# The last FFN norm of a two-layer trunk: its row sums of squares are taken from the turned residual

## Chip, cores and metric

One core of a Trainium2 chip runs the whole program. The metric is the device time of one execution in microseconds: the kernel before took 966.81 us, the median of three runs (966.55 to 966.98).

## What is computed

A decoder trunk of two layers over 512 tokens of 1024 channels, in float32. Each layer adds a mixer and a gated FFN to the residual `h`, each behind an RMS norm:

```
def rms_norm(x, g):
    y = x32 * lax.rsqrt(jnp.mean(x32 * x32, axis=-1, keepdims=True) + EPS)
    return y.astype(x.dtype) * g
...
for layer in range(DEPTH):
    xn = rms_norm(h, norm_mix[layer])
    ...
    h = h + jnp.einsum('bse,ed->bsd', mix, w_out_odd[i])
    hn = rms_norm(h, norm_ffn[layer])
    h = h + gated_conv_ffn(hn, w_ffn_gate[layer], w_ffn_up[layer], ...)
return rms_norm(h, final_norm)
```

The case is about the last `norm_ffn`, that of layer 1: the sum over 1024 channels of the squares of `h`, for each of 512 tokens.

## The kernel before, in words

The residual lies turned: `h[k]` (k = 0 to 7) holds 128 channels on the partitions and all 512 tokens along the free dimension. Every float32 product is made from two parts of each operand, a rounded one (`hi`) and the rest (`lo`), in three matmuls (L156 to L158, or L705 in the FFN's and the projections' block products). ACT makes `hi`; `lo` is made by VectorE as a subtraction (L152, L202, L857), or by ACT and an adding DMA on GpSimd's queue (L141 and L143, L822 to L824).

A `Norm` multiplies h by its gain (`add`, L199, into the pair `hg[k]`) and squares it: ACT squares each `h[k]` (L208, L211), GpSimd adds the seven later squares onto the first (L212). The norm's scale is not needed before a projection, since it is the same for a whole token and is multiplied in behind the products. `rstd_cols` (L225) reduces over the partitions: for each of the four token tiles a product of the summed squares with a column of ones (L229). The root and its refinement follow on [128, 4] (`inv_sqrt`, `newton`: L245 to L255), and `rstd_spread` (L219, L222) turns the four columns into a tile over all tokens.

Around the change the program goes as follows.

- The end of mixer1, `project_blocks` (L614): the right half of the output projection as seven block products. Products 1, 6, 7 and 4 accumulate into one bank for each of two halves, `10a` and `11a`; after each of them VectorE adds what stands in the bank to `h` (L663), so the next one waits for that addition. After the last one `add` makes `hg[4]` to `hg[7]`.
- `ffn1` (L1343) begins with `Ffn.direct` (L769): the first two gate and the first two up tiles, 8 steps i of four products (`gu`). The call `before(i, j)` in it turns the residual: in steps 0 and 1, `turn_residual` (L1354) transposes four blocks of h into a bank `hT` on PE (L1357) and ACT copies it into `y[t]` (L1359): token tile t, left half of the channels (half 0) or right (half 1). Later the down projection is added to y, and the final norm works on it. At step (3, 0) `rstd_cols` is called, at (6, 0) `rstd_spread`.
- Then `block_sums(kp)`, kp = 0 to 3 (L799): ACT scales h into a tile `t1_kp` (L804), VectorE makes sums and differences (L808 to L812), ACT splits them into `t41`, `t23` (L822, L824 with adding DMAs L823 for kp = 0 and 1; L856, L857 for 2 and 3). The tiles share three buffers, so the fourth block sum takes over that of the first. `prepare(2)` (L857, L877 to L900) makes weight sums for the next two hidden tiles, and `products` multiplies them (`g_2a`, `u_2a`, ...); ACT copies the result of gate product 6 out of its bank (L944) before product 7 accumulates on.

PSUM has seven banks for all of this and one (`aux`) for small things. The order of instructions on each engine is set by the tile framework's list scheduler, within what the data allow; places marked `inorder` and `behind` are pinned. Two lines have to be seen for the steps of the change:

```
if (i, j) == (3, 0):
    nc.vector.tensor_copy(self.cols, self.norm.rstd_cols(inorder))
elif (i, j) == (6, 0):
    self.r = self.norm.rstd_spread(inorder)
```

Of the kernel before, what the change touches and what calls it, by code (L numbers as in the profile page):

```python
# [8 lines left out]
F32 = mybir.dt.float32  # L9
F32R = mybir.dt.float32r  # L10
BF16 = mybir.dt.bfloat16
AF = mybir.ActivationFunctionType
ALU = mybir.AluOpType
PSUM = bass.MemoryType.PSUM

P = 128
D = 1024
S = 512
NK = D // P
NT = S // P  # L20
# [4 lines left out]
PAD = 16  # L25
# [6 lines left out]
def tile_trunk(ctx: ExitStack, tc: tile.TileContext, x, norm_mix, norm_ffn, final_norm,  # L32
# [3 lines left out]
    nc = tc.nc  # L36
# [5 lines left out]
    tp = ctx.enter_context(tc.tile_pool(name="tp", bufs=2))  # L42
# [3 lines left out]
    def mm_bank(name):  # L46
        return ps_mm.tile([P, 512], F32, tag="mm", name=name)

    def aux_bank(name):
        return ps_aux.tile([P, 512], F32, tag="aux", name=name)  # L50
# [16 lines left out]
    ones = small[:, :1]  # L67
# [124 lines left out]
    class Norm:  # L192


        def __init__(self, name, gain):
            self.name, self.gain, self.n = name, gain, 0
            self.ssq = tp.tile([P, S], F32, tag="ssq", bufs=1, name=f"ssq_{name}")

        def add(self, k):  # L199
            g = self.gain(k)  # L200
            nc.scalar.activation(hg[k][0], h[k], AF.Copy, scale=g)  # L201
            nc.vector.scalar_tensor_tensor(hg[k][1], h[k], g, hg[k][0].bitcast(F32),  # L202
                                           op0=ALU.mult, op1=ALU.subtract)
            self.square(k)

        def square(self, k, order=lambda ins: ins):
            if self.n == 0:
# [16 lines left out]

        def rstd_cols(self, order=lambda ins: ins):  # L225

            ps = aux_bank(f"ssc_{self.name}")
            for t in range(NT):
                order(nc.tensor.matmul(ps[:, t : t + 1], self.ssq[:, t * P : (t + 1) * P],  # L229
                                       ones, start=True, stop=True))  # L230
            self.cols = inv_sqrt_cols(ps[:, :NT], NT, f"{self.name}c")
            return self.cols

    root_ends = {}
# [15 lines left out]
    def inv_sqrt(r, ss, n, name):  # L250

        ms = work("ms", n, name)
        nc.vector.tensor_scalar(ms, ss, 1.0 / D, EPS, op0=ALU.mult, op1=ALU.add)
        newton(ms, n, name, r)
        return nc.vector.scalar_tensor_tensor(r, ms, 1.5, r, op0=ALU.add, op1=ALU.mult)  # L255

    def inv_sqrt_cols(ss, n, name):
        r = tp.tile([P, LINE], F32, tag="rc", name=f"rc_{name}")[:, :n]
        root_ends[name] = inv_sqrt(r, ss, n, name)
        return r  # L260
# [455 lines left out]
    class Ffn:  # L716
# [195 lines left out]
        def products(self, f, stat):  # L912
# [23 lines left out]
            def after(key, product, bank):  # L936
                halves = range(1 + in_both(key, product))
                if product in onto:
                    ins = add(dst[key, onto[product]], bank, halves)
                    if product == 7:  # L940
                        self.added[key] = ins
                elif (key, product) != ("u", 4):
                    d = dst[key, 7 if product == 5 else product]
                    nc.scalar.copy(d, bank[:, :HALF])  # L944
                    add(d, bank, halves[1:])
# [33 lines left out]
            if in_both("u", 4):  # L979
                last = kept[:, 0, :]  # L980
                nc.scalar.copy(last, bank[:, :HALF])
                add(last, bank, (1,))
# [360 lines left out]
    def ffn1(norm):  # L1343
        with tc.tile_pool(name="f1", bufs=1) as ap:
# [5 lines left out]
            acts = ffn.acts  # L1350
            y = [ap.tile([P, D], F32, name=f"y{t}") for t in range(NT)]
            ssf = ap.tile([P, NT, PAD], F32, name="ssf")

            def turn_residual(t, half):  # L1354
                ps = mm_bank(f"hT{t}_{half}")
                for i in range(4):
                    nc.tensor.transpose(ps[:, i * P : (i + 1) * P],  # L1357
                                        h[half * 4 + i][:, t * P : (t + 1) * P], ident)
                return nc.scalar.copy(y[t][:, half * 512 : (half + 1) * 512], ps)  # L1359

            def before(i, j):
                if i < 2 and j % 2 == 0:
                    turn_residual(j, i)
                    ins = turn_residual(j + 1, i)
                    if (i, j) == (1, 0):
                        ffn.first_sums = ins
# [254 lines left out]
    n = ffn0(n)  # L1621
    n = mixer1(n)
    ffn1(n)


# [28 lines left out]
```

## Time and profile before

| | |
|---|---|
| median of three runs | 966.81 us |
| the profiled execution, its own time | 966.66 us |
| its span, first to last instruction | 964.9 us |
| PE busy | 956.6 us (99%), 5155 instructions |
| VectorE (DVE) busy | 847.2 us (88%), 1435 |
| ScalarE (ACT) busy | 620.8 us (64%), 944 |
| GpSimd (POOL) busy | 162.4 us (17%), 183 |
| mean granted TensorE clock | 0.999 |

The busy shares are averages over the span. The chain of work that ended last is 99% PE. The stretch that the change touches lies between 594 and 664 us of the span. In timeline rows, the first number is the start in us, the second the length of the group, `x4` the number of instructions in it, and in brackets stands the engine's idle time ahead of it and what ended it. An instruction's start may come before the end of the one ahead, since they are pipelined: what one costs its engine is the distance to the next start.

### The profile page before, as it was taken

What the parts mean: (1) busy time and instruction counts of PE and PEld (TensorE: products, weight loads), DVE (VectorE), ACT (ScalarE), POOL (GpSimd) and SP (SyncE); (2) the same over time, 40 slices, a digit from 0 to 9 for tenths busy, and PEclk for the clock granted to TensorE, in tenths of its full rate; (3) what the DMA queues carried; (4) which work ended last, traced back from release to release, by engine and by line L of the source; (5) the groups of instructions that cost most, each with busy time, mean ns of one, the idle gap of its engine ahead of it and who ended that gap; (6) DMA issues with size and microseconds to landing.
All of it is one profiled execution on the core that took longest, in us unless ns stands there. A gap on an engine that the chain in (4) does not pass through costs nothing.

```text
span 964.9 us, 14240 instructions
## 1 busy us (share of the span) xinstructions
PE 956.6 (99%) x5155; PEld 826.5 (86%) x5155; DVE 847.2 (88%) x1435; ACT 620.8 (64%) x944; POOL 162.4 (17%) x183
## 2 busy tenths in 40 slices
PE   9999999999999999999999999999999999999997
PEld 7888898998888888888888888989888888888885
DVE  6887988989899998998878689889998989989898
ACT  5524667766576565765487847787765566646676
POOL 2142333111011010110311002321111011110124
PEclk9999999999999999999999999999999999999999
DMA  7442345777777578774452323467776777667865
GB/s 253 146 141 87 66 144 120 179 188 178 176 174 176 153 175 197 164 180 137 131 153 88 109 88 88 138 134 184 186 181 175 182 176 174 167 168 177 207 146 152
DMA packets 95538, 150.47 MB, mean 156 GB/s; under 512 B 5252, under 2 KB 61548, under 8 KB 95468
## 3 DMA queue, kind: packets, MB, share of 16 engines
q1 hardware_dynamic: 77996, 98.69, 32.8%
q0 software_dynamic: 15696, 49.03, 27.8%
q10 hardware_dynamic: 1776, 1.84, 0.6%
q8 instruction: 41, 0.67, 0.3%
q14 instruction: 29, 0.24, 0.1%
HBM read 98.42 MB, written 2.10 MB: 104 GB/s over the span
## 4 chain that ended last, share of the span: by engine, by line
PE 99%; DMA 0%; DVE 0%; issue 0%; SPq 0%; ACT 0%; DVEq 0%
PE dn L156 3%; PE d L157 3%; PE d L156 3%; PE dn L157 3%; PE d L158 3%; PE dn L158 3%; PE vu_a L1166 2%; PE gu L156 2%; PE gu L158 2%; PE gu L157 2%; PE u_2a L705 1%; PE g_2a L705 1%; PE u_4a L705 1%; PE g_6a L695 1%; PE u_12a L695 1%; PE u_16a L695 1%
## 5 line engine op out<-in xcount | busy, mean ns | idle before, releaser
L143 POOL DMA_DIRECT2D wlo_g<-raw_g x20 | 17.2, 860 | 318.8 <-ACT wlo_g L141 66.5
L741 DVE SCALAR_TENSOR_TENSOR c<-rows,prm,c 128x512 f32<-128x512 f32 x88 | 64.9, 746 | 1.2 <-ACT c L739 1.0
L156 PE MATMUL d<-a_hi,whi_d 128*128 128x512 f32 x144 | 56.1, 389 | 0.0
L156 PE MATMUL dn<-whi_dn,a_hi 128*128 128x512 f32 x144 | 56.1, 389 | 0.0
L157 PE MATMUL d<-a_lo,whi_d 128*128 128x512 f32 x144 | 56.1, 389 | 0.0
L157 PE MATMUL dn<-wlo_dn,a_hi 128*128 128x512 f32 x144 | 56.0, 389 | 0.0
L158 PE MATMUL d<-a_hi,wlo_d 128*128 128x512 f32 x144 | 56.0, 389 | 0.0
L158 PE MATMUL dn<-whi_dn,a_lo 128*128 128x512 f32 x144 | 56.0, 389 | 0.0
L856 ACT ACTIVATE whi_a<-raw_g 128x512 fp32r<-128x512 f32 x20 | 12.6, 632 | 67.2 <-PE g_18e L695 9.4
L739 ACT ACTIVATE c<-rows,prm 128x512 f32<-128x512 f32 x44 | 31.3, 714 | 10.2 <-DVE rows L968 10.1
L1371 DVE SCALAR_TENSOR_TENSOR y<-dn,small,y 128x512 f32<-128x512 f32 x40 | 28.0, 749 | 6.7 <-PE dn L158 6.7
L749 ACT ACTIVATE s<-c,prm 128x512 f32<-128x512 f32 x44 | 31.4, 715 | 3.2 <-DVE c L741 3.0
L265 ACT ACTIVATE a_hi<-s 128x512 fp32r<-128x512 f32 x40 | 24.7, 626 | 12.2 <-PE d L158 9.4
L201 ACT ACTIVATE hg<-h,prm 128x512 fp32r<-128x512 f32 x24 | 17.2, 719 | 23.5 <-DVE h L314 17.0
L158 PEld LDWEIGHTS dn<-whi_dn,a_lo 128*128 128x128 f32 x144 | 27.0, 188 | 5.7
L158 PEld LDWEIGHTS d<-a_hi,wlo_d 128*128 128x128 f32 x144 | 27.0, 188 | 5.6
L157 PEld LDWEIGHTS dn<-wlo_dn,a_hi 128*128 128x128 f32 x144 | 27.0, 188 | 5.6
L156 PEld LDWEIGHTS d<-a_hi,whi_d 128*128 128x128 f32 x144 | 27.0, 188 | 5.6
L156 PEld LDWEIGHTS dn<-whi_dn,a_hi 128*128 128x128 f32 x144 | 27.0, 188 | 5.6
L157 PEld LDWEIGHTS d<-a_lo,whi_d 128*128 128x128 f32 x144 | 27.0, 188 | 5.5
L141 ACT ACTIVATE wlo_g<-raw_g 128x1024 fp32r<-128x1024 f32 x20 | 21.0, 1048 | 16.3 <-PE g_2e L705 7.6
L152 DVE TENSOR_TENSOR wlo_d<-raw_d,whi_d 128x1024 fp32r<-128x1024 f32 x18 | 22.0, 1224 | 10.4 <-ACT whi_d L151 10.4
(1279 smaller groups left out, 3377.6 us busy)
## 6 DMA issues: line engine op xcount, KB each, us to landing
raw_g<-in_w_ffn_gate_dram SPq DMA_DIRECT2D x40, 512.0 KB, 3.8
raw_u<-in_w_ffn_up_dram SPq DMA_DIRECT2D x40, 512.0 KB, 3.7
raw_dn<-in_w_ffn_down_dram SPq DMA_DIRECT2D x22, 512.0 KB, 3.5
wlo_g<-raw_g POOLq DMA_DIRECT2D x20, 512.0 KB, 5.2
wlo_u<-raw_u POOLq DMA_DIRECT2D x20, 512.0 KB, 6.1
raw_d<-in_w_ffn_down_dram SPq DMA_DIRECT2D x18, 512.0 KB, 4.1
wlo_s12g<-s12g POOLq DMA_DIRECT2D x18, 512.0 KB, 6.6
wlo_s34g<-s34g POOLq DMA_DIRECT2D x18, 512.0 KB, 6.2
```

The source lines that it names most:

```text
L141: first = nc.scalar.activation(lo, raw, AF.Copy, scale=-1.0)
L152: behind(nc.vector.tensor_tensor(lo, raw, hi.bitcast(F32), ALU.subtract), after[0])
L156: nc.tensor.matmul(ps, lhs[0], rhs[0], start=start, stop=False, skip_group_check=skip)
L157: nc.tensor.matmul(ps, lhs[0], rhs[1], start=False, stop=False, skip_group_check=skip)
L158: nc.tensor.matmul(ps, lhs[1], rhs[0], start=False, stop=stop, skip_group_check=skip)
L265: nc.scalar.activation(hi, src, AF.Copy, scale=scale)
L695: last_matmul[0] = nc.tensor.matmul(ps if low else banks[at], left(kp)[low], right(kp)[0] if low else both(kp), start=first, stop=kp == NP ...
L705: nc.tensor.matmul(ps, l, r, start=first, stop=end, skip_group_check=True)
L739: nc.scalar.activation(c, t[:, 0:S], AF.Copy, scale=prm("cf", ft))
L741: self.last_conv = nc.vector.scalar_tensor_tensor(c, t[:, i : S + i], prm("cf", i * NF + ft), c, op0=ALU.mult, op1=ALU.add)
L749: self.last_silu = nc.scalar.activation(s, c, AF.Silu, bias=self.prm("bf", ft))
L1371: return nc.vector.scalar_tensor_tensor(dst, ps, ffn.cols[:, t : t + 1], dst, op0=ALU.mult, op1=ALU.add)
```

## The change

The norm `f1` (the last FFN norm) no longer squares the turned `h`; its `ssq` tile, eight squares on ACT, seven additions on GpSimd and four products with the column of ones are gone. Instead `turn_residual` squares each piece of `y[t]`, the residual with tokens on the partitions, as soon as it has been copied: the left halves by ACT's Square with a row sum (`accum_out`), the right halves by VectorE's scalar_tensor_tensor with a row sum. `row_sums` adds the two halves, [128, 4], and the root starts from there. The other norms are as before.

```
-        def __init__(self, name, gain):
+        def __init__(self, name, gain, total=None):
             self.name, self.gain, self.n = name, gain, 0
-            self.ssq = tp.tile([P, S], F32, tag="ssq", bufs=1, name=f"ssq_{name}")
+            self.total = total
+            if name != "f1":
+                self.ssq = tp.tile([P, S], F32, tag="ssq", bufs=1, name=f"ssq_{name}")
...
-            self.square(k)
+            if self.name != "f1":
+                self.square(k)
...
-            ps = aux_bank(f"ssc_{self.name}")
-            for t in range(NT):
-                order(nc.tensor.matmul(ps[:, t : t + 1], self.ssq[:, t * P : (t + 1) * P],
-                                       ones, start=True, stop=True))
-            self.cols = inv_sqrt_cols(ps[:, :NT], NT, f"{self.name}c")
+            if self.total is not None:
+                ss = self.total()
+            else:
+                ss = aux_bank(f"ssc_{self.name}")[:, :NT]
+                for t in range(NT):
+                    order(nc.tensor.matmul(ss[:, t : t + 1], self.ssq[:, t * P : (t + 1) * P],
+                                           ones, start=True, stop=True))
+            self.cols = inv_sqrt_cols(ss, NT, f"{self.name}c")
...
+            ssy = ap.tile([P, 2, PAD], F32, name="ssy")
...
-                return nc.scalar.copy(y[t][:, half * 512 : (half + 1) * 512], ps)
+                dst = y[t][:, half * 512 : (half + 1) * 512]
+                ins = nc.scalar.copy(dst, ps)
+                sq = tp.tile([P, S], F32, tag="sq", name=f"sqy{t}_{half}")
+                at = ssy[:, half, t : t + 1]
+                if half == 0:
+                    nc.scalar.activation(sq, dst, AF.Square, accum_out=at)
+                else:
+                    nc.vector.scalar_tensor_tensor(sq, dst, 1.0, dst, op0=ALU.mult, op1=ALU.mult,
+                                                   accum_out=at)
+                return ins
+
+            def row_sums():
+                nc.vector.tensor_tensor(ssy[:, 0, :NT], ssy[:, 0, :NT], ssy[:, 1, :NT], ALU.add)
+                return ssy[:, 0, :NT]
+
+            norm.total = row_sums
```

The scheduler then orders some neighbours anew. Line numbers in rows of the changed kernel are those of that kernel: what was L663 is L669 there, L152 stays, L202 is L204, L705 is L711, L804 is L810, L822 and L824 are L828 and L830, L1357 and L1359 are L1364 and L1367. The first place is the end of mixer1 on PE; `11_4` are the weights of block product 4, `01_7` those of product 7. Before, and then in the changed kernel:

```order
L705 MATMUL oo1_11a_5813<-t43_1_5687,whi_oo1_11_4_5795 128x256 x2
L705 MATMUL oo1_11a_5813<-t43_1_5687,wlo_oo1_11_4_5796 128x256
L1357 MATMUL hT0_0_6048<-ident_79,h0_103 128x128
L1357 MATMUL hT0_0_6048<-ident_79,h1_104 128x128
L1357 MATMUL hT0_0_6048<-ident_79,h2_105 128x128
L1357 MATMUL hT0_0_6048<-ident_79,h3_106 128x128
```

```order
L711 MATMUL oo1_11a_5802<-t43_1_5686,whi_oo1_01_7_5780 128x256 x2
L711 MATMUL oo1_11a_5802<-t43_1_5686,wlo_oo1_01_7_5781 128x256
L1364 MATMUL hT0_0_6026<-ident_79,h0_103 128x128
L1364 MATMUL hT0_0_6026<-ident_79,h1_104 128x128
L1364 MATMUL hT0_0_6026<-ident_79,h2_105 128x128
L1364 MATMUL hT0_0_6026<-ident_79,h3_106 128x128
```

The first eight transposes of the residual have moved from behind product 4 to between product 7 and product 4.

The second place is VectorE at the same time; the first addition to `h6` and that to `h7` here are those of product 7 (banks `10a` and `11a`), `wlo_u1_0_1` is the low part of an FFN weight. Before, then changed:

```order
L202 TENSOR_SCALAR hg4_115<-h4_107,prm1_4631,hg4_115 128x512
L663 TENSOR_TENSOR h6_109<-oo1_10a_5799,h6_109 128x256
L202 TENSOR_SCALAR hg5_116<-h5_108,prm1_4631,hg5_116 128x512
L663 TENSOR_TENSOR h7_110<-oo1_11a_5813,h7_110 128x256
L152 TENSOR_TENSOR wlo_u1_0_1_6045<-raw_u1_0_1_6041,whi_u1_0_1_6044 128x1024
```

```order
L204 TENSOR_SCALAR hg4_115<-h4_107,prm1_4631,hg4_115 128x512
L152 TENSOR_TENSOR wlo_u1_0_1_6023<-raw_u1_0_1_6019,whi_u1_0_1_6022 128x1024
L204 TENSOR_SCALAR hg5_116<-h5_108,prm1_4631,hg5_116 128x512
L669 TENSOR_TENSOR h6_109<-oo1_10a_5788,h6_109 128x256
L669 TENSOR_TENSOR h7_110<-oo1_11a_5802,h7_110 128x256
```

The addition to h6 has moved behind the weight split and hg5; on ACT the split's first half, `whi_u1_0_1` (L151), has moved up likewise, between hg4 and hg5.

The third place is ACT in `direct`; `y0` to `y3` are the token tiles, `t1_0` is the first block sum, `t41` and `t23` its splits. Before, then changed:

```order
L201 ACTIVATE hg7_118<-h7_110,prm1_4631 128x512
L211 ACTIVATE sq_f17_6008<-h7_110 128x512
L1359 COPY y2_6017<-hT2_0_6068 128x512
L1359 COPY y3_6018<-hT3_0_6074 128x512
L1359 COPY y0_6015<-hT0_1_6088 128x512
L1359 COPY y1_6016<-hT1_1_6094 128x512
L822 ACTIVATE t41_1_0_6226<-t1_0_6218 128x512
L824 ACTIVATE t41_1_0_6226<-t1_0_6218 128x512
L822 ACTIVATE t23_0_6224<-t1_0_6218 128x256
```

```order
L1371 ACTIVATE sqy2_0_6056,ssy_5997<-y2_5994 128x512
L1371 ACTIVATE sqy3_0_6064,ssy_5997<-y3_5995 128x512
L1367 COPY y0_5992<-hT0_1_6074 128x512
L1367 COPY y1_5993<-hT1_1_6082 128x512
L810 ACTIVATE t1_0_6208<-h0_103,prm1_4631 128x512
L1367 COPY y2_5994<-hT2_1_6096 128x512
L1367 COPY y3_5995<-hT3_1_6104 128x512
L810 ACTIVATE t1_1_6226<-h1_104,prm1_4631 128x512
L810 ACTIVATE t1_2_6244<-h2_105,prm1_4631 128x512
L141 ACTIVATE wlo_g1_2_1_6295<-raw_g1_2_1_6278 128x1024
L251 ACT_TABLE_LOAD
L251 ACTIVATE sd_f1c_6134<-ms_f1c_6132 128x4
```

The first block sum (L804, now L810), which stood ahead of hg7, has moved behind the first two copies of the right half, and its splits have moved from behind those copies to behind the root (`sd`): the last row shown is followed by them. On VectorE the four squares (L1373) stand ahead of the first block sum's additions, but for the first of these, which stands between the second and the third square.

## The prediction

> **What bounds the kernel now.** I looked first at what TensorE (PE) waited for, in the view of waits:
>
> ```profile
> PE clock L58 <- PEq L1640: 0.8, 1, 0.8
> PE z L417 <- ACT whi_z L410: 0.3, 1, 0.3
> ```
>
> The columns are who waited, for whom, the total, how often and the longest. These two rows are the whole list: 1.1 us, at the very start, in an execution of 966.66 us. So the end is set by the sum of what PE issues, and an edit can move the time in two ways only: PE gets less to issue, or PE begins to wait where today everything arrives in time. ScalarE (ACT), VectorE (DVE) and GpSimd (POOL) count only through the moments at which they hand something to PE.
>
> **First term: what PE no longer issues.** The timeline of PE around the products with the column of ones (L229), columns start, length, engine, line, operation:
>
> ```profile
> 629.37 0.39 PE L158 MATMUL gu<-hg,wlo_u 128*128 128x512 f32 x1
> 629.60 0.95 PE L229 MATMUL ssc_f<-small,ssq_f 128*128 128x1 f32 x8
> 630.40 0.49 PE L156 MATMUL gu<-hg,whi_g 128*128 128x512 f32 x1
> 630.73 0.40 PE L157 MATMUL gu<-hg,whi_g 128*128 128x512 f32 x1
> ```
>
> From the start of the L158 row to that of the L157 row it is 630.73 - 629.37 = 1.36 us. Without the eight records between, these are two ordinary steps of 0.23 (629.37 to 629.60), 0.46. The products cost PE 1.36 - 0.46 = 0.90 us, and nothing hides them: **-0.90**.
>
> **Second term: product 4 behind a later addition.** The list scheduler moves eight transposes of the residual (L1357) ahead of both halves of product 4:
>
> ```profile
> 614.93 0.40 PE L705 MATMUL oo_10a<-t,whi_oo 128*128 128x256 f32 x2
> ...
> 617.81 1.03 PE L1357 MATMUL hT<-ident,h 128*128 128x128 f32 x8
> 618.60 0.47 PE L156 MATMUL gu<-hg,whi_g 128*128 128x512 f32 x1
> ```
>
> They take 618.60 - 617.81 = 0.79, so product 4 can start at 614.93 + 0.79 = 615.72. It writes on into the bank that DVE reads in the addition of product 7 (h6, L663), and must wait for that addition. Before, the addition stood at 613.71; now the weight split wlo_u (L152) and hg5 stand ahead of it. The rows of ACT, then those of DVE:
>
> ```profile
> 612.28 0.72 ACT L201 ACTIVATE hg<-h,prm 128x512 fp32r<-128x512 f32 x1 [1.97 <-DVE h L663]
> ...
> 614.57 1.05 ACT L151 ACTIVATE whi_u<-raw_u 128x1024 fp32r<-128x1024 f32 x1
> ```
>
> ```profile
> 610.70 1.21 DVE L152 TENSOR_TENSOR wlo_g<-raw_g,whi_g 128x1024 fp32r<-128x1024 f32 x1
> ...
> 613.04 0.75 DVE L202 SCALAR_TENSOR_TENSOR hg<-h,prm,hg 128x512 fp32r<-128x512 f32 x1 [0.36 <-ACT hg L201]
> 613.71 0.42 DVE L663 TENSOR_TENSOR h<-oo_10a,h 128x256 f32<-128x256 f32 x1
> ...
> 615.77 1.98 DVE L152 TENSOR_TENSOR wlo_u<-raw_u,whi_u 128x1024 fp32r<-128x1024 f32 x1
> ```
>
> ACT's hg4 starts at 612.28 or a little earlier (it waited for DVE); I take 611.95. whi_u follows at once, 0.62 later, without the square between: 612.6 to 613.6. Then DVE: wlo_u 1.2, hg5 0.67 (613.04 to 613.71), the addition 0.42: 615.9. PE waits 615.9 - 615.72 = 0.2; starting from 612.28 it is 0.5, and with half a length earlier nothing. **+0.2**, bounds 0 and +0.6.
>
> The lengths without a neighbour (1.21, 0.75) are used because POOL's additions are gone from here:
>
> ```profile
> 613.67 3.00 POOL L212 TENSOR_TENSOR ssq_f<-ssq_f,sq_f 128x512 f32<-128x512 f32 x2 [8.90 <-ACT sq_f L211]
> ...
> 629.74 0.86 POOL L143 DMA_DIRECT2D wlo_g<-raw_g  x1 [1.61 <-ACT wlo_g L141]
> 631.63 2.66 POOL L823 DMA_DIRECT2D t<-t  x3 [1.03 <-ACT t L822]
> ```
>
> Beside the first of these rows wlo_u took 1.98 where wlo_g took 1.21. [...]
>
> **Third term: the block sums come late.** On ACT the new squares stand ahead of the splits of the first block sums (L822, L824). What ACT does from hg7 to the fourth block sum (L804) stays one unbroken queue:
>
> ```profile
> 620.83 0.73 ACT L201 ACTIVATE hg<-h,prm 128x512 fp32r<-128x512 f32 x1
> 621.45 0.62 ACT L211 ACTIVATE sq_f<-h 128x512 f32<-128x512 f32 x1
> 621.97 2.06 ACT L1359 COPY y<-hT 128x512 f32<-128x512 f32 x4
> ...
> 626.54 0.43 ACT L822 ACTIVATE t<-t 128x256 fp32r<-128x256 f32 x1
> 626.85 0.43 ACT L824 ACTIVATE t<-t 128x256 fp32r<-128x256 f32 x1
> ...
> 634.35 0.71 ACT L804 ACTIVATE t<-h,prm 128x512 f32<-128x512 f32 x1
> ...
> 652.66 0.37 ACT L944 COPY rows<-g_2a 128x256 f32<-128x256 f32 x1
> ```
>
> A square that also writes its sum exists already, in mixer1:
>
> ```profile
> 505.15 0.63 ACT L1073 ACTIVATE sqv<-v 128x512 f32<-128x512 f32 x1
> 505.67 0.20 ACT L1073 ACTIVATION_READ_ACCUMULATOR sqv<-v 128x1 f32 x1
> 505.77 0.63 ACT L1073 ACTIVATE sqv<-v 128x512 f32<-128x512 f32 x1
> ```
>
> One costs 505.77 - 505.15 = 0.62. hg7 now starts near 619.95, since its square and that of hg6 no longer stand before it. Up to the fourth block sum ACT gains four squares (+2.48) and one block sum that stood ahead of hg7 (+0.62), and loses one square (621.97 - 621.45 = 0.52): 634.35 - 0.88 + 2.48 + 0.62 - 0.52 = 636.0.
>
> It then finds its buffer taken. The fourth block sum reuses the first one's buffer, and that is free when the first's three DMAs have landed. Their sources are now written behind the squares and the root. Between the third source and the fourth block sum ten splits stand in the order, seven of 0.31 (626.85 - 626.54) and three twice as wide, some 0.52 as the square: 3.7. So the third source is there at 636.0 - 3.7 = 632.3, and POOL, which takes 0.89 for each (2.66 / 3), issues the third DMA half of that later, at about 632.75, right behind the large DMA wlo_g. How long such a DMA takes to land, for the ones issued 632 to 633 just behind wlo_g, min, median and max:
>
> ```profile
> DMA to landing us min/median/max: 4.2/4.3/4.4
> ```
>
> 632.75 + 4.3 = 637.1, **2.75 later** than the 634.35 of before. What follows is one chain handed to and fro between ACT and DVE with a single gap in it:
>
> ```profile
> 642.78 0.69 DVE L788 TENSOR_TENSOR rows<-gu,rstd_f 128x512 f32<-128x512 f32 x1 [0.67 <-PE gu L158]
> ```
>
> The 0.67 takes up part of it, which leaves 2.0 to 2.1; the copy of gate product 6 (L944, row 652.66), behind silu and a split on ACT, comes about 1.95 later, from 654.6 to 655.0. PE's product 7 accumulates into the bank that this copy reads:
>
> ```profile
> 654.69 0.40 PE L705 MATMUL g_2a<-t,whi_s34g 128*128 128x256 f32 x2
> ```
>
> PE will be there at 654.69 - 0.90 + 0.2 = 654.0. It waits 655.0 - 654.0 = **+1.0**. Bounds: a landing sooner by 1 us leaves no wait, and below zero it cannot go, since PE has no other wait to lose; the upper end, +3.3, is the second rival's. I take +1.0 because the nearest rows (4.2 to 4.4) have the same DMA ahead.
>
> **What costs nothing.** The eight squares on ACT and the seven additions on POOL fed only the removed products. The last addition of the root (128x4) on DVE and the root itself end near 632, and the transposes that spread it on PE are called only at step (6, 0), three steps of twelve matmuls behind the removed products: that is the cover, and a wait there would need it gone. POOL's queue loses seven rows, and wlo_g now stands ahead of the first block sum's DMAs, which is counted above. SP's queue is the same.
>
> **Sum.** 966.66 - 0.90 + 0.2 + 1.0 = 966.96. The median of the three runs, 966.81, is 0.15 above the profiled execution, so against the runs it is 967.1; I say **967.0**.
>
> **The rivals.** *The gain stands.* The DMAs land 1 us sooner, or ACT and DVE close the gap, and PE waits nowhere: 966.66 - 0.90 = 965.8. For it: no wait of PE in today's profile. Against it: the slack at product 7 is 654.69 - 653.03 (652.66 + 0.37) = 1.66, less the 0.90 that PE is earlier, 0.76; the chain is 1.95 later.
>
> *VectorE's squares are slow.* No instruction in this trace squares on DVE with a sum written. Four of them stand in DVE's queue ahead of the first block sum's additions, which the splits on ACT need. The nearest row has two f32 inputs from SBUF and no sum:
>
> ```profile
> L741 DVE SCALAR_TENSOR_TENSOR c<-rows,prm,c 128x512 f32<-128x512 f32 x88 | 64.9, 746 | 1.2 <-ACT c L739 1.0
> ```
>
> The squares can begin when ACT has copied the right half of the first row tile, about 624.6 (619.95, then 0.62 for hg7, 1.24, 1.0, 1.24 and 0.5 for squares and copies). Four at 0.67, and some 2.1 of additions between and behind them, end at 629.4, while ACT reaches the first split at 630.1: hidden. So DVE is last from 0.18 more per square on, 0.93 each. At twice the 0.746 they end 4 x 0.75 = 3.0 later, 632.4, the first split starts 2.3 later, and all of it arrives at product 7 or a product ahead of it: 966.96 + 2.3 = 969.3, slower by 0.26%. [...]
>
> **How the numbers follow.** The forecast (waits at product 4 and at product 7 that about eat up the gain, 966.3 to 967.9): 0.56. The gain stands (965.6 to 966.2): 0.20. Slow squares (968.0 to 969.4): 0.18. Something that I don't see, to either side: 0.06. The range takes in all three with the bounds of their terms: 965.6 to 969.4. A difference of 0.2%, 1.93 us, is about what a measurement of this kernel can tell from no change. Faster than 964.9 needs more than the whole first term: 0.02. Slower than 968.7 needs the second rival at three quarters of its price or more (0.10 of its 0.18), or an unseen wait: 0.12. Within: 0.86.
>
> **What would show it.** Right: L229 of this norm is gone from PE; product 4 waits 0 to 0.6 for DVE h; the fourth block sum (L810 in the changed kernel) starts near 637 after waiting for a DMA; g_2a product 7 waits about 1 us for ACT's copy. Wrong: PE's list of waits is as short as before (first rival), or the squares on DVE take over 1 us each (second). What I trust least is the 2 us lag handed on through twenty instructions of ACT and DVE: a gap that I overlooked would take the wait at product 7 away.

## The result, and the profile after

The changed kernel takes **969.84 us** (median of 7 runs, 969.21 to 970.87) beside 966.81 us (966.53 to 967.04) of the kernel before: 0.32% slower, ratio 1.0032, 95% interval 1.0023 to 1.0042. The prediction said 967.0 and at most 969.4. The profiled execution has a span of 968.4 us, 3.5 more than before.

The view of PE's waits, changed kernel:

```profile
PE clock L58 <- PEq L1662: 0.8, 1, 0.8
PE g_2a L711 <- ACT rows L950: 0.8, 1, 0.8
PE oo_10a L711 <- DVE h L669: 0.2, 1, 0.2
```

The two forecast waits are there, at the places and nearly at the sizes named, and no others. They come to 1.0 us; 3.5 us are lost. So the first thing to read is where PE falls behind. Its timeline at the three places of the prediction: product 4, the place of the removed products, and product 7.

```profile
615.15 1.03 PE L1364 MATMUL hT<-ident,h 128*128 128x128 f32 x8
616.35 0.47 PE L711 MATMUL oo_10a<-t,whi_oo 128*128 128x256 f32 x2 [0.16 <-DVE h L669]
...
619.29 0.40 PE L156 MATMUL gu<-hg,whi_g 128*128 128x512 f32 x1
...
629.96 0.39 PE L158 MATMUL gu<-hg,wlo_u 128*128 128x512 f32 x1
630.18 0.39 PE L156 MATMUL gu<-hg,whi_g 128*128 128x512 f32 x1
...
655.19 0.51 PE L711 MATMUL g_2a<-t,whi_s34g 128*128 128x256 f32 x2 [0.76 <-ACT rows L950]
```

Right behind product 7 of mixer1, PE stands at 615.15, where it stood at 614.93 before: 0.22 later, ahead of anything that the change touches. From there:

- Product 4 starts 1.20 after the transposes begin, 0.41 more than their 0.79: PE could have gone on at 615.94, VectorE's addition to h6 (its row stands below the list) ends at 616.21, and PE starts 0.14 after that. The next gate product stands at 619.29, before at 618.60: +0.69, so the move cost 0.69 - 0.22 = **0.47** (0.16 of it counted as a wait).
- Between 629.96 and 630.18 there is now one ordinary step. The gate product that was at 630.40 is at 630.18: -0.22, so the removed products gave 0.69 + 0.22 = **0.91**.
- Product 7 of g_2a was at 654.69 and is at 655.19: +0.50, so its wait cost about **0.7**.

```profile
615.79 0.42 DVE L669 TENSOR_TENSOR h<-oo_10a,h 128x256 f32<-128x256 f32 x1
```

Since the change began that is 0.50 - 0.22 = +0.28; the prediction's sum was +0.3. ACT behind it, the fourth block sum and the copy of gate product 6:

```profile
637.33 0.73 ACT L810 ACTIVATE t<-h,prm 128x512 f32<-128x512 f32 x1 [0.80 <-DMA t<-t]
...
654.76 0.38 ACT L950 COPY rows<-g_2a 128x256 f32<-128x256 f32 x1
```

The block sum waits for a DMA and starts at 637.33 (forecast 637.1), the copy ends at 655.14 (forecast 655.0). VectorE's new squares:

```profile
625.73 0.69 DVE L1373 SCALAR_TENSOR_TENSOR sqy<-y 128x512 f32<-128x512 f32 x1
626.34 0.08 DVE L1373 DVE_READ_ACCUMULATOR sqy<-y 128x1 f32 x1
626.34 0.48 DVE L814 SCALAR_TENSOR_TENSOR t<-h,prm,t 128x256 f32<-128x256 f32 x1
```

One costs 626.34 - 625.73 = 0.61 us, far from the 0.93 at which the second rival begins.

So up to 655 us the prediction holds. At the end PE is not 0.5 but 3.4 us late (its last matmul starts at 960.99, before at 957.55), without a wait in between. What can still differ is the matmul itself. The down projection (`dn`, L156 to L158) in one group of 48 consecutive products without a gap, its first and its last row; the kernel before, then the changed one:

```profile
836.50 0.39 PE L156 MATMUL dn<-whi_dn,a_hi 128*128 128x512 f32 x1
...
847.16 0.39 PE L158 MATMUL dn<-whi_dn,a_lo 128*128 128x512 f32 x1
```

```profile
838.67 0.39 PE L156 MATMUL dn<-whi_dn,a_hi 128*128 128x512 f32 x1
...
849.58 0.40 PE L158 MATMUL dn<-whi_dn,a_lo 128*128 128x512 f32 x1
```

47 steps take 10.66 us before and 10.91 after: 226.8 against **232.1 ns a step**, the same instructions in the same order. There are 432 of them (3 x 144), 432 x 5.3 ns = **2.3 us**. The clock is not it: 0.999 granted in both executions.

### The profile page after: what moved, and what is told of

Same layout as the page of the kernel before. It is cut to its first block, busy times and chain, and to the rows that moved or that the text cites. A ratio compares the mean times of both kernels' runs of the same rounds, so it can differ in the third digit from the quotient of the medians.

```text
span 968.4 us, 14229 instructions
## 1 busy us (share of the span) xinstructions
PE 959.5 (99%) x5147; PEld 826.9 (85%) x5147; DVE 844.7 (87%) x1444; ACT 619.6 (64%) x944; POOL 151.8 (16%) x176
## 4 chain that ended last, share of the span: by engine, by line
PE 98%; DVE 1%; ACT 0%; issue 0%; DVEq 0%; ACTq 0%
PE dn L157 3%; PE dn L158 3%; PE dn L156 3%; PE d L156 3%; PE d L158 3%; PE d L157 3%; PE vu_a L1172 2%; PE gu L156 2%; PE gu L158 2%; PE gu L157 2%; PE u_4a L711 1%; PE u_10a L701 1%; PE u_12a L701 1%; PE u_8a L701 1%; PE u_20a L701 1%; PE u_18a L701 1%
## 5 line engine op out<-in xcount | busy, mean ns | idle before, releaser
L158 PE MATMUL dn<-whi_dn,a_lo 128*128 128x512 f32 x144 | 56.8, 395 | 0.0
L156 PE MATMUL dn<-whi_dn,a_hi 128*128 128x512 f32 x144 | 56.8, 394 | 0.0
L156 PE MATMUL d<-a_hi,whi_d 128*128 128x512 f32 x144 | 56.1, 390 | 0.0
L158 PE MATMUL d<-a_hi,wlo_d 128*128 128x512 f32 x144 | 56.0, 389 | 0.0
L158 PEld LDWEIGHTS dn<-whi_dn,a_lo 128*128 128x128 f32 x144 | 27.1, 188 | 6.3
L156 PEld LDWEIGHTS dn<-whi_dn,a_hi 128*128 128x128 f32 x144 | 27.1, 188 | 6.2
L158 PEld LDWEIGHTS d<-a_hi,wlo_d 128*128 128x128 f32 x144 | 27.0, 188 | 5.7
L156 PEld LDWEIGHTS d<-a_hi,whi_d 128*128 128x128 f32 x144 | 27.0, 188 | 5.5
L152 DVE TENSOR_TENSOR wlo_d<-raw_d,whi_d 128x1024 fp32r<-128x1024 f32 x18 | 22.0, 1223 | 9.4 <-ACT whi_d L151 9.4
```

The costliest lines, as they stand in the source:

```text
L152: behind(nc.vector.tensor_tensor(lo, raw, hi.bitcast(F32), ALU.subtract), after[0])
L156: nc.tensor.matmul(ps, lhs[0], rhs[0], start=start, stop=False, skip_group_check=skip)
L158: nc.tensor.matmul(ps, lhs[1], rhs[0], start=False, stop=stop, skip_group_check=skip)
```

## The experiments

**What they test.** The change has a line that no step of the prediction priced: `ssy = ap.tile([P, 2, PAD], F32, name="ssy")`, a new tile of 2 x 16 x 4 = 128 bytes a partition. The tiles of the last FFN that are laid behind it (block sums, their splits `t41`, `c`, `s`, `a_hi`, `a_lo`) all move up by 128 bytes. The splits `t23` don't: in this layer they take over the buffers of `h`. Rows name `t41` and `t23` alike `t`. In the kernel before, `h`, `hg`, the weights and the activations start at the same place within 256 bytes: the first `whi` at byte 90752, the first `a_hi` of this FFN at 206720, 453 x 256 bytes on. In the changed kernel that `a_hi` is at 206848.

A matmul has two operands, and in the traces two records: an LDWEIGHTS of 128x128 (432 in `dn`, 188 ns each before) and a MATMUL of 128x512 or 128x256. The second operand that a row names is that of the LDWEIGHTS, called loaded below; the first, 512 or 256 columns wide, is called streamed: for `ssc_f<-small,ssq_f` (L229 before) the MATMUL is 128x1, like the column of ones out of `small`, and the LDWEIGHTS 128x128, like a token tile of `ssq_f`. In `dn` the weights are streamed and `a_hi`, `a_lo` are loaded; with `hg` and `t` in the gate and up products it is the other way round. *Distance* below is the start of the loaded operand minus that of the streamed one, modulo 256 bytes.

The theory is that the distance between the two operands sets the step. Its rival is the new order: PSUM banks given out in another turn, ACT and DVE running later beside PE. Each group of `dn` is read as above, from its first row to its last, 47 steps on.

**e1: the kernel before, with a gap of 128 bytes.** The order of every engine is that of before.

```diff
             ssf = ap.tile([P, NT, PAD], F32, name="ssf")
+            gap = ap.tile([P, 2, PAD], F32, name="gap")
```

> The kernel before with one unused 128-byte tile laid where the change lays ssy, so that every later tile of the last FFN (a_hi, a_lo, the block sums and their splits) lies 128 bytes further; the order of all engines is that of before. Placement theory (the time is lost because the down projection's operands lie 128 bytes further): the 2.9 us that the changed kernel loses after 655 us come with it, 966.8 + 2.9 = 969.7, and the step between two dn matmuls goes from 227 to about 232 ns. Rival (it is lost to the new order: PSUM banks handed out in another turn, or ACT and DVE running later beside PE): 966.8, and the step stays at 227.

Measured: 970.27 us (969.27 to 971.30, 5 runs), ratio 1.0036 (1.0024 to 1.0049) to its 966.71.

```profile
837.49 0.39 PE L156 MATMUL dn<-whi_dn,a_hi 128*128 128x512 f32 x1
...
848.40 0.40 PE L158 MATMUL dn<-whi_dn,a_lo 128*128 128x512 f32 x1
```

10.91 us, 232.1 ns. An unused tile alone brings the whole loss (3.6 us, where 2.9 were expected); the rival falls.

**e2: the change, without moving a tile.** The sums go to 16 unused columns of `small`.

```diff
-            ssy = ap.tile([P, 2, PAD], F32, name="ssy")
+            ssy = small[:, 2 * PAD : 3 * PAD].rearrange("p (a b) -> p a b", a=2)
```

> The changed kernel with its row sums kept in 16 unused columns of the tile small, so that no tile of the last FFN moves; the order is that of the changed kernel. Placement theory: what is left is the sum of the terms, -0.9 for the products, +0.2 at product 4, +0.8 at product 7, so 966.8 + 0.1 = 966.9, and dn steps of 227 ns. Rival (new order): 969.8 and 232 ns, as the changed kernel.

Measured: 967.11 us (966.65 to 967.61, 11 runs), ratio 1.0004 (0.9995 to 1.0013): no difference from before, and where the prediction put the change. The waits:

```profile
PE g_2a L711 <- ACT rows L950: 1.0, 1, 1.0
PE clock L58 <- PEq L1662: 0.8, 1, 0.8
PE oo_10a L711 <- DVE h L669: 0.2, 1, 0.2
```

Product 7 waits the 1.0 us of the forecast. What the change says it does is worth nothing; its 128 bytes cost 2.7 us (969.84 - 967.11).

**e3: the change with a tile of 256 bytes.**

```diff
-            ssy = ap.tile([P, 2, PAD], F32, name="ssy")
+            ssy = ap.tile([P, 2, 2 * PAD], F32, name="ssy")
```

> The changed kernel with ssy twice as wide, so that the later tiles lie 256 bytes further than before instead of 128. Placement theory, if it is the place within 256 bytes that counts: as with no shift, 966.9, dn steps of 227 ns. If any move away from the old distance counts: 969.8. Rival (new order): 969.8.

Measured: 967.19 us (966.72 to 967.73, 11 runs), ratio 1.0005 (0.9996 to 1.0014). A larger move costs nothing if it is 256 bytes: what counts was the same again 256 bytes on (226.6 ns a step in `dn`).

**e4, e10, e11: the kernel before with gaps of 64, 32 and 192 bytes**, in the place of e1's.

```diff
+            gap = ap.tile([P, PAD], F32, name="gap")
...
+            gap = ap.tile([P, 8], F32, name="gap")
...
+            gap = ap.tile([P, 48], F32, name="gap")
```

> The kernel before with an unused tile of 64 bytes in the same place. Placement theory, if only starts on a multiple of 256 bytes are slow: 966.8. If every start other than the old one within 256 bytes is slow: 969.7. Rival (new order): 966.8, since the order is that of before.

> The kernel before with an unused tile of 32 bytes where the change lays ssy: a_hi, a_lo and the split sums lie 32 bytes off. Distance theory (any distance that is no multiple of 256 bytes is slow for 128x512): dn steps of 232 to 234 ns, 966.8 + 2.3 to 2.9 = 969.1 to 969.7. Rival (a multiple of 32 bytes is enough; slow only from 64 on): 966.8, 227 ns.

> The kernel before with an unused tile of 192 bytes where the change lays ssy. Distance theory: dn steps of 232 to 234 ns as with 64 and 128 bytes, 969.1 to 969.9. Rival (the cost grows from 0 with the distance and falls to 0 only at 256): between the two, dn steps of 229 to 231 ns, about 968.

The groups of `dn`, for 64, 32 and 192 bytes:

```profile
837.56 0.39 PE L156 MATMUL dn<-whi_dn,a_hi 128*128 128x512 f32 x1
...
848.53 0.40 PE L158 MATMUL dn<-whi_dn,a_lo 128*128 128x512 f32 x1
```

```profile
837.96 0.40 PE L156 MATMUL dn<-whi_dn,a_hi 128*128 128x512 f32 x1
...
848.93 0.40 PE L158 MATMUL dn<-whi_dn,a_lo 128*128 128x512 f32 x1
```

```profile
836.94 0.39 PE L156 MATMUL dn<-whi_dn,a_hi 128*128 128x512 f32 x1
...
847.71 0.39 PE L158 MATMUL dn<-whi_dn,a_lo 128*128 128x512 f32 x1
```

| distance in `dn` | step, ns | time, us | ratio to before |
|---|---|---|---|
| 0 (before) | 226.8 | 966.7 | |
| 32 (e10) | 233.4 | 969.89 | 1.0035 (1.0022 to 1.0047) |
| 64 (e4) | 233.4 | 969.30 | 1.0028 (1.0017 to 1.0039) |
| 128 (e1) | 232.1 | 970.27 | 1.0036 (1.0024 to 1.0049) |
| 192 (e11) | 229.1 | 967.89 | 1.0012 (1.0003 to 1.0020) |

32 bytes are already slow; at 192 the rival of e11 was right, the cost is only a third. The curve isn't symmetric: 64 and 192 are as far from 0, yet differ by 4 ns. The times don't follow the step of `dn` alone: at 64 it is as long as at 32, yet the time is the lower one. `t41` moved as well, and what became of its products stands under e6. Why e1 lies above both stays open; its profiled execution, 969.27 us, is the fastest of its five.

The group view shows the last case only if all three lines of the product are read. At 192 their mean lengths are 394, 392 and 389 ns, where each was 389 before; L156 alone would show nothing:

```profile
L158 PE MATMUL dn<-whi_dn,a_lo 128*128 128x512 f32 x144 | 56.8, 394 | 0.0
L157 PE MATMUL dn<-wlo_dn,a_hi 128*128 128x512 f32 x144 | 56.4, 392 | 0.0
L156 PE MATMUL dn<-whi_dn,a_hi 128*128 128x512 f32 x144 | 56.0, 389 | 0.0
```

The ends of matmuls in the profile are modelled, so the step is taken from starts.

**e5: everything moved by 64 bytes.** This tells distance from place.

```diff
     cp = ctx.enter_context(tc.tile_pool(name="cp", bufs=1))
+    gap = cp.tile([P, PAD], F32, name="gap")
```

> The kernel before with an unused tile of 64 bytes ahead of all others, so that every tile of the program lies 64 bytes further and all distances between tiles stay. Distance theory (TensorE is slow when its two operands, the loaded 128x128 piece and the streamed 128x512 one, lie apart by other than a multiple of 256 bytes): 966.8, dn steps of 227 ns. Rival (the place itself counts, a start of 128 within 256 bytes being the fast one): all 128x512 products lie as badly as dn did with the 64-byte gap, 6.4 ns for each of about 2500, 966.8 + 16 = 983, with d as well as dn at 233 ns.

Measured: 967.01 us (966.02 to 968.62, 11 runs), ratio 1.0003 (0.9994 to 1.0012).

```profile
836.73 0.39 PE L157 MATMUL dn<-whi_dn,a_hi 128*128 128x512 f32 x1
...
847.38 0.39 PE L159 MATMUL dn<-whi_dn,a_lo 128*128 128x512 f32 x1
```

10.65 us, 226.6 ns: the place by itself does nothing.

**e6: the weights and all later tiles moved by 64 bytes, `h` and `hg` not.**

```diff
+    gp = ctx.enter_context(tc.tile_pool(name="gp", bufs=1))
+    gap = gp.tile([P, PAD], F32, name="gap")
     wp = ctx.enter_context(tc.tile_pool(name="wp", bufs=1))
```

> The kernel before with an unused tile of 64 bytes between h, hg and the rest: the weights, the activations a_hi and a_lo and all later tiles move by 64 bytes, hg and h stay. Distance theory: d and dn, whose operands both moved, stay at 227 ns; the products of hg with a weight (about 910 of 128x512) go to some 233 ns, 910 x 6.4 ns = 5.8 us, 966.8 + 5.8 = 972.6. Rival (the place itself counts): d and dn slow as well, above 980.

Measured: 967.39 us (966.89 to 968.70, 11 runs), ratio 1.0007 (0.9998 to 1.0015), far below the 972.6 expected, and farther still from the rival's 980. The rows say why. 96 consecutive products of `hg` with a weight in the first mixer, before and in e6:

```profile
54.44 0.39 PE L156 MATMUL av<-hg,whi_av 128*128 128x512 f32 x1
...
75.98 0.39 PE L158 MATMUL av<-hg,wlo_av 128*128 128x512 f32 x1
```

```profile
55.67 0.39 PE L158 MATMUL av<-hg,whi_av 128*128 128x512 f32 x1
...
77.83 0.39 PE L160 MATMUL av<-hg,wlo_av 128*128 128x512 f32 x1
```

95 steps in 21.54 and in 22.16 us, 226.7 and 233.3 ns: the step that `dn` has at the same distance in e4. `dn` and `d` stay at 227, both operands having moved. So far as expected. But the products of 256 columns went the other way; 12 of a block product in the first FFN, before and in e6:

```profile
177.34 0.40 PE L705 MATMUL u_2b<-hg,whi_u 128*128 128x256 f32 x2
...
178.66 0.28 PE L705 MATMUL u_2b<-hg,wlo_u 128*128 128x256 f32 x1
```

```profile
179.82 0.40 PE L707 MATMUL u_2b<-hg,whi_u 128*128 128x256 f32 x2
...
181.09 0.28 PE L707 MATMUL u_2b<-hg,wlo_u 128*128 128x256 f32 x1
```

11 steps in 1.32 and in 1.27 us: 120.0 and 115.5 ns. What the 512-wide products lost, the 256-wide ones of the FFNs mostly gave back: summed over the steps of both whole traces, 5.3 us lost and 4.6 gained. The expectation also took all 910 products at 6.4 ns; where `hg` is the loaded operand the distance is -64, that is 192, and `v` lost 2.3 (47 steps from 484.24 to 495.00, 228.9 ns; before 483.02 to 493.67, 226.6), as `dn` at 192 in e11.

The gaps of e1, e4, e10 and e11 say more on this width, since they moved `t41` too. It is streamed, so its distance is 256 less the gap. Twelve of its products of 256 columns, before (distance 0) and in e11 (distance 64):

```profile
651.81 0.40 PE L705 MATMUL u_2e<-t,whi_s12u 128*128 128x256 f32 x2
...
653.13 0.28 PE L705 MATMUL u_2e<-t,wlo_s12u 128*128 128x256 f32 x1
```

```profile
651.83 0.40 PE L705 MATMUL u_2e<-t,whi_s12u 128*128 128x256 f32 x2
...
653.09 0.28 PE L705 MATMUL u_2e<-t,wlo_s12u 128*128 128x256 f32 x1
```

11 steps take 1.32 us at 0 and 1.26 at 64; at 128 (e1), 192 (e4) and 224 (e10) they take 1.30. So this group gains at each distance that was run, and most at 64.

**e7: the change, with `c`, `s`, `a_hi` and `a_lo` moved on to 256 bytes.** The block sums and splits stay 128 bytes off.

```diff
             c = ap.tile([P, S], F32, tag="c", bufs=2, name=f"c{n}")
...
+            if n == "1_0":
+                gap = ap.tile([P, 32], F32, name="gap")
```

(The added lines stand ahead of the first.)

> The changed kernel with an unused tile of 128 bytes ahead of c: the block sums and their splits stay 128 bytes off, but c, s, a_hi and a_lo lie 256 bytes from their old place. Distance theory: dn back at 227 ns, which gives back 432 x 5.3 ns = 2.3 us of the 2.9; the products of the splits t (128x512, 2.0 ns each) stay slow: 969.8 - 2.3 = 967.5. Rival (it is not a_hi and a_lo, but the block sums, c or y and the engines that write them): dn stays at 232 ns, 969.8.

Measured: 967.83 us (967.42 to 969.01, 11 runs), ratio 1.0010 (1.0001 to 1.0019).

```profile
836.90 0.40 PE L156 MATMUL dn<-whi_dn,a_hi 128*128 128x512 f32 x1
...
847.60 0.39 PE L158 MATMUL dn<-whi_dn,a_lo 128*128 128x512 f32 x1
```

10.70 us, 227.7 ns: all but 0.9 of the 5.3 ns are back. Of the 2.7 us, 2.0 (969.84 - 967.83) come from `a_hi` and `a_lo`, and 0.7 (967.83 - 967.11) are left. Of these some 0.4 (432 x 0.9 ns) are still in `dn`, whose operands are at distance 0; in e3, where the block sums and splits moved by 256 too, it took 226.6. So the two that a matmul reads are not quite all that counts, and why stays open. The rest, some 0.3, fits the slower products of the splits.

**e8: the sums in `small`, and all eight squares on VectorE.** This tests the cause of the wait at product 7.

```diff
-                if half == 0:
-                    nc.scalar.activation(sq, dst, AF.Square, accum_out=at)
-                else:
-                    nc.vector.scalar_tensor_tensor(sq, dst, 1.0, dst, op0=ALU.mult, op1=ALU.mult,
-                                                   accum_out=at)
+                nc.vector.scalar_tensor_tensor(sq, dst, 1.0, dst, op0=ALU.mult, op1=ALU.mult,
+                                               accum_out=at)
```

> The changed kernel with the row sums in small (no tile moved) and all eight squares on VectorE, which stands idle for 3.1 us ahead of its first square. Theory (the wait at product 7 comes from the four squares that stand on ACT ahead of the block sums): that wait of 0.8 us goes, product 4's 0.2 stays or goes, 966.8 - 0.9 + 0.2 = 966.1. Rival (the late block sums come from the splits' place behind the root, or VectorE gets too late with 8 x 0.61 us): a wait of about 0.8 us stays at product 7 or another product, 966.9 to 967.1 as with the sums in small alone.

Measured: 966.16 us (965.65 to 967.33, 11 runs), ratio 0.9992 (0.9983 to 1.0001).

```profile
PE clock L58 <- PEq L1659: 0.8, 1, 0.8
PE oo_10a L711 <- DVE h L669: 0.2, 1, 0.2
```

```profile
633.87 0.71 ACT L810 ACTIVATE t<-h,prm 128x512 f32<-128x512 f32 x1
...
652.44 0.36 ACT L950 COPY rows<-g_2a 128x256 f32<-128x256 f32 x1
```

The fourth block sum starts 3.5 us sooner than in the changed kernel and waits for nothing, the copy comes 2.3 sooner, and product 7's wait is gone. The scheduler also put the first block sum and its splits further forward here, so the squares' place and theirs aren't told apart; together they are the cause.

**e9: e8, and `hg` 64 bytes from the weights in the FFNs alone.** The version that e6 points to: the FFNs' block products are mostly 256 wide. All other pairs keep the distance 0, except, against what was expected, the products with `t23` in layer 1: `t23` lies in the buffers of `h`, which stay where they were while the weights move. The same holds in e6.

```diff
-    hg2 = [cp.tile([P, 2, S], F32R, name=f"hg{k}") for k in range(NK)]
-    hg = [(t[:, 0], t[:, 1]) for t in hg2]
+    hg_all = cp.tile([P, NK * 2 * S + PAD], F32R, name="hg")
+
+    def hg_at(off):
+        return [hg_all[:, off + k * 2 * S : off + (k + 1) * 2 * S]
+                .rearrange("p (a s) -> p a s", a=2) for k in range(NK)]
+
+    hg, hg2 = hg_at(PAD), hg_at(0)
+    hg, hg_f = ([(t[:, 0], t[:, 1]) for t in ts] for ts in (hg, hg2))
...
+            hg_ = hg_f if self.name[0] == "f" else hg
```

> The kernel with all squares on VectorE and the sums in small, and besides hg as one tile that is 64 bytes longer: the two FFN norms and their products use it from its start, the mixers from byte 64 on, and all later tiles move by 64 bytes. So hg and the weights lie 64 bytes apart in the FFNs alone; every other pair keeps its distance. Distance theory, from the kernel with the weights moved by 64: there the 256-wide products of hg ran at 114.5 instead of 119.3 ns a step, the 512-wide at 233, and the FFNs came out 1.2 (layer 0) and 0.5 us (layer 1) ahead: 966.2 - 1.7 = 964.5. Rival (what the 256-wide products gain there came from other pairs that moved): 966.2 or more, above all because gu and the other 512-wide products lose 6 ns each.

Measured: **964.52 us** (963.99 to 965.69, 10 runs), ratio 0.9978 (0.9968 to 0.9987) to its 966.75: 2.23 us under the kernel before, where e8 is 0.48 under with an interval that reaches 1, and so faster than both kernels.

```profile
654.09 0.39 PE L718 MATMUL u_2b<-hg,whi_u 128*128 128x256 f32 x2
...
655.34 0.28 PE L718 MATMUL u_2b<-hg,wlo_u 128*128 128x256 f32 x1
```

11 steps in 1.25 us, 113.6 ns, against 120.0 at distance 0. The 512-wide `gu` runs at 233 ns a step, as the rival said, but the 256-wide products gain more. It is the gain of `hg`: the products of `t` in layer 1, from e8 to e9, win and lose about alike (408 of 256 columns step by 117.0 for 119.3 ns, 276 of 512 by 232.0 for 229.2).

## Why the prediction was wrong, point by point

- **"What PE no longer issues", -0.90:** right, 0.91.
- **"Product 4 behind a later addition", +0.2, bounds 0 and 0.6:** right in its place and cause, 0.47 in size: the addition ended 0.27 after PE was there, and the 0.14 from its end to PE's start was in no term. The reading that GpSimd's additions had lengthened wlo_u fits too: without them it took 1.23 us in the changed kernel, not 1.98.
- **"The block sums come late", +1.0:** right down to the buffer and the DMA; 0.7 in the profile of the changed kernel, 1.0 waited in e2's. e8 took this wait away. The chain through some twenty instructions, which was trusted least, held within 0.25 us.
- **"The gain stands":** did not happen, since both waits came. **"VectorE's squares are slow":** did not happen, 0.61 us each. Its 969.3 us rests on twice the 0.746 us of the row without a sum. No run shows the factor of two; with the same f32 tile as both sources, the square with its sum is 0.69 long, the mean of that row 0.746.
- **The step that failed** is the first one: "an edit can move the time in two ways only: PE gets less to issue, or PE begins to wait". There is a third: the same matmuls, issued without a wait, each take longer. The 128 bytes of `ssy` moved the loaded operand of 432 products away from distance 0, 5.3 ns each, and the streamed operand of others; 2.7 us in all (e2 against the change). Of the rest only the second term was mis-sized, by 0.27 us: with the tiles left in place the kernel takes 967.11, where 967.0 was forecast. "Something that I don't see" had a chance of 0.06.

That 969.3, the price of the slow squares, lies near the measured time is chance: the runs give that rival no part of it.

Open is why the distance matters. That it does, e1, e5 and e6 together say: 232.1 ns a step in `dn` with the loaded operand moved by 128 bytes, 226.6 with both moved by 64, and in `av` 233.3 for 226.7 with the loaded one alone moved by 64. What makes it so, no run here shows. Nor is the distance all: in the kernel before, where every pair of these is at 0, the 276 products of `t` of 512 columns in the last FFN average 229.2 ns a step (read from their starts), not 226.8. Nor was it tried whether `hg` at other distances than 0 and 64 would gain more in the FFNs, or what holds for other types than f32.

## What to carry to other kernels

When PE is the bound and a change allocates, widens or drops a tile, look at what the tiles behind it become for TensorE: compare the step between starts of the same matmul group, before and after, not only waits and counts. A new small tile goes into free columns of an old one (967.11 us in e2, beside 969.84) or is filled up to 256 bytes (967.19 in e3); a place with nothing behind it was not run. And when a profile loses time without a wait, find the row from which PE drifts; a loss that grows with the count of one product is a price per instruction (here 432 times 5.3 ns).

## What the runs showed of the hardware that was not expected

- The step of a 128x512 f32 product depends on the distance of its two operands modulo 256 bytes; in `dn` 226.8 ns at 0, 233.4 at 32 and 64, 232.1 at 128, 229.1 at 192, 226.6 again at 256 (e3: 47 steps from 836.77 to 847.42). Moving both alike changes nothing (e5: 226.6).
- The 128x256 products of the groups read were faster off 0: in `u_2b` 113.6 to 115.5 ns at 64, 120.0 at 0; in `u_2e` 114.5 at 64 and some 118 at 128, 192 and 224, 120.0 at 0. So a distance of 64 suits these and slows the 512-wide `dn`.
- VectorE's square with a row sum, both sources the same f32 tile, takes 0.61 us for 128x512, less than the 0.67 (613.04 to 613.71 before) of the instruction on two tiles, without a sum, that makes hg5.
